# Two store and load cuts in a dilated 3x3 convolution: the first pair's stores regrouped, the eighth pair's load halved

## The chip, the cores and the metric

The kernel runs on one core of a Trainium2 chip. The metric is the device time of one execution in microseconds (us); several executions are made in rounds, the kernel before and the other kernel on the same chip. Two kernels count as the same when they are within 2%. All ratios below are ratios of means: the mean time of one kernel's fast runs over the mean of the other's fast runs of the same rounds, so a ratio is not quite the ratio of the medians quoted beside it. Runs over 1.5% above the fastest of the same kernel are left out of the ratios. They are not left out of the medians: where a median contains one, it is a little high.

## The reference, cut to what matters

```python
batch, c_in, h, w, c_out, k, dilation = 16, 64, 64, 64, 128, 3, 2      # float32
x_pad = np.pad(x, ((0, 0), (0, 0), (2, 2), (2, 2)))
# for all b, co, ci, kh, kw:
output[b, co] += weight[co, ci, kh, kw] * x_pad[b, ci, kh*2:kh*2+h, kw*2:kw*2+w]
```

The input is 16.8 MB, the output 33.6 MB. Nearly all of both has to cross between HBM and the on-chip memory once.

## The kernel before

Two images make a pair, because 2 x 64 input channels fill the 128 partitions. There are 8 pairs. One load brings a pair (128 partitions x 64 rows x 64 columns, 2 MB). Each pair is computed in four groups `g` of 16 rows; `G` counts all 32 groups. ACT casts the input to fp16, DVE forms row sums, PE does the products (with sums shared between rows), DVE adds them into the output tile `osb`. An output tile holds both images of a pair: 128 output channels x 2 images x 4096 values, 4 MB. There are three input buffers and three output buffers. All loads and stores are issued by SP, in program order, so they form one queue.

```python
    def load(pb, cuts=(0, H)):
        x32_tiles[pb] = fpool.tile([P, HW], f32, tag="x32", name="x32")
        for lo, hi in zip(cuts[:-1], cuts[1:]):
            nc.sync.dma_start(
                out=x32_tiles[pb][:, lo * W : hi * W], in_=x_pair[pb, :, lo * W : hi * W]
            )
    # ... cut: casts, row sums, weights; ahead of the loop load(0), load(1), load(2)

    def store(pb, m, r0=0, r1=H, rows=((0, P),)):
        for lo, hi in rows:
            nc.sync.dma_start(
                out=out_img[2 * pb + m, lo:hi, r0 * W : r1 * W],
                in_=o_tiles[pb][lo:hi, m * HW + r0 * W : m * HW + r1 * W],
            )

    FOUR = ((0, P - 4), (P - 4, P))
    ROWS4 = 8

    for G in range(ngroups):
        # ... cut: the products and the sums of group g of pair pb
        if G == 0:
            load(XF)                                   # XF = 3
        if g == NG - 1 and 0 < pb < npairs - XF - 1:
            load(pb + XF + 1)
        if pb in (0, npairs - 1):
            if g % 2 == 1:
                store(pb, 0, (g - 1) * GR, (g + 1) * GR)
                if pb and g == 1:
                    store(pb, 1, 0, 2 * GR - ROWS4)
                    store(pb, 1, 2 * GR - ROWS4, 2 * GR, FOUR)
                else:
                    store(pb, 1, (g - 1) * GR, (g + 1) * GR)
            if G == NG - 1:
                load(XF + 1)
        elif g == NG - 1:
            store(pb, 0)
            store(pb, 1)
```

So the first pair is stored in four transfers of 1 MB (rows 0 to 31 of each image after the second group, rows 32 to 63 after the fourth), and every later pair but the last in two transfers of 2 MB.

## Time and profile before

| | before |
|---|---|
| time | 126.86 us (126.79 to 127.05, 3 runs) |
| span of the profiled run | 125.0 us |
| PE's last matmul ends | 107.8 us |
| DVE's last addition ends | 109.1 us |
| moved by DMA | 50.8 MB, 406 GB/s over the span |

The page of the profile, kernel before. In the second block each character or number is one of 40 slices of 3.1 us: the mean busy share of the 16 DMA engines in tenths, and what they moved in GB/s.

```profile
span 125.0 us, 2339 instructions
...
DMA  4999999899999999999999999999999999999991
GB/s 145 373 427 456 435 420 399 299 425 422 446 438 430 425 420 440 422 430 420 435 425 433 430 430 430 420 425 425 446 430 425 430 420 425 425 433 411 424 387 76
DMA packets 4466, 50.78 MB, mean 406 GB/s; under 512 B 488, under 2 KB 488, under 8 KB 1000
...
PE 76%; DMA 6%; ACT 2%; DVE 1%; DVEq 1%; SPq 1%; issue 0%
```

The two readings seem to disagree. The chain of waits follows the work back from the last instruction, and gives PE 76%. But nothing computes after 109.1 us, and the span ends at 125.0. In those 16 us the DMA engines write out what was queued, at about the rate that they have had since the third slice. The chain follows releases between instructions; a queue that always has a backlog does not appear in it as a wait. The DMA row is the one to read here: apart from the first and the last slice it is at nine tenths throughout, with one weak slice, the eighth (299 GB/s).

The DMA issues of SP around the places that the change touches, kernel before (timeline of SP; a row can merge several issues, and its duration then runs to the end of the last of them):

```profile
16.62 7.04 SPq L185 DMA_DIRECT2D out_dram<-osb  x4
23.76 0.61 SPq L64 DMA_DIRECT2D x<-in_x_dram  x1
...
54.70 0.34 SPq L64 DMA_DIRECT2D x<-in_x_dram  x1
```

Two of the four stores are issued at 16.6 us and two at 22.6. The fifth load follows at 23.8.

### The profile page before, as it was taken

To read this page: it belongs to the slowest core of one execution; us is meant where nothing else is said; L and a number is where in the kernel's file an instruction comes from. 1 tells how busy PE (TensorE), PEld (TensorE's weight loads), DVE (VectorE), ACT (ScalarE), POOL (GpSimd) and SP (SyncE) were. 2 spreads that over 40 slices of the span, in tenths; PEclk is the share of its full clock that TensorE was granted. 3 is DMA by queue.
4 is the path that set the end of the run, shared out by engine and by line. 5 is a ranking of instruction groups with operands and counts; after the bars stand their busy time and mean duration, and the time that the engine had idled before them with its cause. 6 is when DMAs were issued, how large, how long until landed. Compare 5 with 4: busy or idle time off the path is not lost.

```text
span 125.0 us, 2339 instructions
## 1 busy us (share of the span) xinstructions
PE 105.1 (84%) x1000; PEld 56.0 (45%) x1000; DVE 90.8 (73%) x103; ACT 64.9 (52%) x68; POOL 2.2 (2%) x8
## 2 busy tenths in 40 slices
PE   6996999999999999999999999999999999400000
PEld 2252555555555555555555555555555555200000
DVE  0562998988898888988988898888988987700000
ACT  4287996665666566656665666566653333000000
POOL 2400000000000000000000000000000000000000
PEclk9999999999999999999999999999999999985555
DMA  4999999899999999999999999999999999999991
GB/s 145 373 427 456 435 420 399 299 425 422 446 438 430 425 420 440 422 430 420 435 425 433 430 430 430 420 425 425 446 430 425 430 420 425 425 433 411 424 387 76
DMA packets 4466, 50.78 MB, mean 406 GB/s; under 512 B 488, under 2 KB 488, under 8 KB 1000
## 3 DMA queue, kind: packets, MB, share of 16 engines
q1 hardware_dynamic: 4456, 50.63, 96.6%
q8 instruction: 8, 0.13, 0.4%
q14 instruction: 2, 0.02, 0.0%
HBM read 17.07 MB, written 33.55 MB: 405 GB/s over the span
## 4 chain that ended last, share of the span: by engine, by line
PE 76%; DMA 6%; ACT 2%; DVE 1%; DVEq 1%; SPq 1%; issue 0%
PE psA L171 31%; PE psB L171 30%; PE psP L171 16%; DMA x<-in_x_dram 6%; ACT x L73 2%; DVE osb L234 1%; DVEq L290 1%; ACT p_sb L227 1%; SPq L64 0%; SPq L88 0%; DVEq L234 0%
## 5 line engine op out<-in xcount | busy, mean ns | idle before, releaser
L171 PEld LDWEIGHTS <-w_sb 64*128 64x128 f16 x960 | 53.9, 94 | 46.6 <-issue 1.5
L227 ACT COPY p_sb<-psP 128x1024 f32<-128x1024 f32 x32 | 32.4, 1012 | 36.8 <-issue 21.6
L234 DVE TENSOR_TENSOR osb<-psA,p_sb 128x1024 f32<-128x1024 f32 x32 | 39.2, 1224 | 13.6 <-PE psA L171 9.0
L171 PE MATMUL psA<-x,w_sb 64*128 64x496 f16 (+3 forms) x384 | 45.0, 365 | 0.0
L171 PE MATMUL psB<-x,w_sb 64*128 64x496 f16 (+3 forms) x384 | 45.0, 365 | 0.0
L234 DVE TENSOR_TENSOR osb<-psB,p_sb 128x1024 f32<-128x1024 f32 x32 | 39.0, 1220 | 0.0
L73 ACT CAST x<-x 128x1024 f16<-128x1024 f32 (+2 forms) x31 | 32.1, 1044 | 0.6 <-DMA x<-in_x_dram 0.5
L171 PE MATMUL psP<-xs,w_sb 64*128 64x496 f16 (+1 forms) x192 | 26.0, 371 | 1.2 <-ACT p_sb L227 1.2
L85 DVE TENSOR_TENSOR xs<-x 128x512 f16<-128x512 f16 x32 | 13.3, 415 | 0.6 <-ACT x L73 0.6
L101 PE MATMUL dm<-zero 128*128 128x512 f16 x10 | 4.6, 580 | 1.2 <-DVE zero L93 1.2
L111 DVE CAST wd<-w 128x192 f16<-128x192 f32 x1 | 0.5, 502 | 2.4 <-DMA w<-in_weight_dram 2.4
L101 PEld LDWEIGHTS <-zero 128*128 128x128 f16 x10 | 1.1, 124 | 2.6 <-issue 1.3
L124 PEld LDWEIGHTS <-wd 128*64 128x64 f16 x30 | 1.0, 118 | 2.2 <-DVE wd L111 1.1
L124 PE MATMUL wt<-ident,wd 128*64 128x128 f16 x30 | 1.6, 241 | 0.2 <-DVE wd L111 0.2
L113 ACT ACT_TABLE_LOAD x1 | 1.3, 1283 | 0.7 <-PEq L276 0.7
L136 ACT CAST w_sb<-wt 128x384 f16<-128x384 f32 x1 | 0.5, 479 | 1.9 <-PE wt L124 1.9
L113 ACT CAST wd<-w 128x192 f16<-128x192 f32 x1 | 0.5, 537 | 1.6 <-DMA w<-in_weight_dram 1.6
L138 DVE CAST w_sb<-wt 128x384 f16<-128x384 f32 x1 | 0.6, 557 | 0.9 <-PE wt L124 0.9
L93 DVE MEMSET zero<- 128x256 uint32 x1 | 0.3, 272 | 0.9 <-PEq L276 0.9
L112 POOL TENSOR_TENSOR wd<-w 128x192 f16<-128x192 f32 x1 | 0.8, 792 | 2.3 <-DMA w<-in_weight_dram 2.3
L115 POOL CAST wd<-w 128x192 f16<-128x192 f32 x1 | 0.8, 803 | 0.0
L114 DVE TENSOR_TENSOR wd<-w 128x192 f16<-128x192 f32 x1 | 0.8, 780 | 0.0
(11 smaller groups left out, 3.6 us busy)
## 6 DMA issues: line engine op xcount, KB each, us to landing
out_dram<-osb SPq DMA_DIRECT2D x12, 2048.0 KB, 19.3
x<-in_x_dram SPq DMA_DIRECT2D x7, 2048.0 KB, 17.6
out_dram<-osb SPq DMA_DIRECT2D x7, 1024.0 KB, 13.5
x<-in_x_dram SPq DMA_DIRECT2D x1, 1088.0 KB, 5.3
x<-in_x_dram SPq DMA_DIRECT2D x1, 960.0 KB, 7.1
out_dram<-osb SPq DMA_DIRECT2D x1, 768.0 KB, 15.9
w<-in_weight_dram SPq DMA_DIRECT2D x1, 288.0 KB, 2.8
out_dram<-osb SPq DMA_DIRECT2D x1, 248.0 KB
```

Source lines behind the costliest of these rows:

```text
L73: nc.scalar.copy(out=x16_tiles[pb][:, lo * W : hi * W], in_=x32_tiles[pb][:, lo * W : hi * W])
L85: nc.vector.tensor_tensor(out=s, in0=v[:, :, 0], in1=v[:, :, 1], op=add)
L101: nc.tensor.matmul(out=dm[:, 0:512], lhsT=zero[:, 0:P], rhs=zero)
L112: nc.gpsimd.tensor_tensor(out=wdv[:, 3], in0=wv[:, 0], in1=wv[:, 1], op=sub)
L113: nc.scalar.copy(out=wdv[:, 2], in_=wv[:, 0])
L114: nc.vector.tensor_tensor(out=wdv[:, 1], in0=wv[:, 2], in1=wv[:, 1], op=sub)
L115: nc.gpsimd.tensor_copy(out=wdv[:, 4], in_=wv[:, 2])
L124: nc.tensor.matmul(out=wts[k % 3][r * CI : (r + 1) * CI, c0 + j * CO : c0 + (j + 1) * CO], lhsT=wd[:, t * CI : (t + 1) * CI], rhs=ident,)
L171: nc.tensor.matmul(out=po, lhsT=w_sb[pp, t * CO : (t + 1) * CO], rhs=rhs, start=first and j == 1, stop=last and j == 2,)
L227: nc.scalar.copy(out=p_sb, in_=psP)
L234: nc.vector.tensor_tensor(out=o[:, :, b0 : b0 + NBLK, e], in0=ps.rearrange("p (m b q) -> p m b q", m=2, q=2 * W), in1=pv, op=add,)
L290: with _tile.TileContext(nc) as tc:
```

## The change

The intent, as it can be read from the source: store the first pair in fewer and mostly larger transfers (1.5 MB for rows 0 to 47 of each image, then 1 MB for rows 48 to 63 of both images together), and cut the eighth pair's load in two, so that its first half can be issued, and land, before the second.

```diff
+    def store_both(pb, r0, r1):
+        nc.sync.dma_start(
+            out=out_img[2 * pb : 2 * pb + 2, :, r0 * W : r1 * W].rearrange("m o q -> o m q"),
+            in_=o_tiles[pb].rearrange("p (m q) -> p m q", m=2)[:, :, r0 * W : r1 * W],
+        )
# ... cut
         if g == NG - 1 and 0 < pb < npairs - XF - 1:
-            load(pb + XF + 1)
-        if pb in (0, npairs - 1):
+            load(pb + XF + 1, (0, H) if pb < 3 else (0, H // 2, H))
+        if G == NG - 2:
+            store(0, 0, 0, (NG - 1) * GR)
+            store(0, 1, 0, (NG - 1) * GR)
+        if G == NG - 1:
+            store_both(0, (NG - 1) * GR, H)
+            load(XF + 1)
+        elif pb == npairs - 1:
             if g % 2 == 1:
                 store(pb, 0, (g - 1) * GR, (g + 1) * GR)
-                if pb and g == 1:
+                if g == 1:
# ... cut: the last pair's stores are unchanged
-            if G == NG - 1:
-                load(XF + 1)
```

## The prediction

> **What bounds the kernel now.** The chain of waits puts 76% of the span on PE, but PE's work ends near 106.7 us and DVE's at 108.0; the span is 125.0. The last 17 us are the DMA queue emptying. The 40 slices show the DMA engines nine tenths busy from the third on, mostly at 420 to 446 GB/s, 50.8 MB in all. The Trainium skill ("DMA: Bandwidth & Descriptors", "Where 436 GB/s comes from") gives a ceiling of 435 GB/s; the stretches 30 to 60 us show 428 to 433, so it agrees. The packets' time is 121.4 us per engine, and the first byte moves at 2.3 us. So the kernel is one saturated queue: its bytes plus three losses: the start, a dip (slice 8, 299 GB/s: about 21.3 to 23.9 us, when the last packets of the fourth load take up to 1.2 us instead of 0.61; 0.96 us of excess per engine), and a tail in which the engines end unevenly, the last some 4 us after the first.
>
> **What the change does, costed by the packet records.** A packet of 8 KB takes 309 ns, one of 16 KB 611: about 7 ns plus 37.75 ns per KB. My estimates from these are 158 ns for 4 KB and 460 for 12 KB.
> - First pair's stores: 512 packets of 8 KB (512 x 309 / 16 = 9.89 us of 16 engines) become 256 of 12 KB and 256 of 4 KB (256 x 618 / 16 = 9.89 us). No difference. Four issues become three, on a sequencer that is idle there.
> - The combined store has 128 partitions as its slowest dimension; the skill (same page, "How many engines (k)") says that such a transfer uses 16 engines. I expect the full rate.
> - Eighth load: 128 packets of 16 KB (4.89 us) become 256 of 8 KB (4.94 us): +0.06 us. One issue more. Its first half waits for only half of the casts that free the buffer, so it can be issued some 6 us before 54.7.
> - Moved: the first stores are issued at about 19.5 us instead of 16.6. By then the queue still holds the fourth load, which lands at about 24 us, so it does not run dry; the second store still comes at 22.6, before the fifth load at 23.8: the queue's order is unchanged. The eighth load took 20.6 us from issue to landing, behind a long backlog; issuing half of it earlier changes no order either.
>
> **On the critical path** (the queue): +0.06 us, and whatever happens to the dip and to the unevenness at the end, each of which could move by half a microsecond. If the dip came from the early stores waiting behind the load it would shrink; I think it more likely stays.
>
> **Prediction.** 126.7 us, 125.9 to 127.4 eight times in ten. Faster by over 2%: 0.02; within 2%: 0.96; slower: 0.02.
>
> **What would show it.** Right: DMA busy nine tenths through 18 to 30 us with no hole, the combined store landing about as late as its predecessors did (near 34 us), PE's end unmoved near 106.7, slice 8 still low. Wrong: a hole in the DMA row before the first stores, the combined store slow or on few engines, DVE waiting longer for out_dram<-osb (0.5 us now), or slice 8 at 420 GB/s (then about 1 us faster).
>
> **What would make it wrong.** The halves or the later stores shifting the engines against each other, so that the tail gets longer or shorter; or 4 KB packets being slower than estimated.

## More of the kernel before

The timeline of the end, kernel before (start, duration, engine, line, operation):

```profile
106.49 1.29 PE L171 MATMUL psB<-x,w_sb 64*128 64x512 f16 x12
...
107.91 1.21 DVE L234 TENSOR_TENSOR osb<-psB,p_sb 128x1024 f32<-128x1024 f32 x1
109.16 0.93 SPq L185 DMA_DIRECT2D out_dram<-osb  x2
```

## The result, and the profile after

| | before | after |
|---|---|---|
| time | 126.87 us (126.79 to 127.05, 4 runs) | 126.68 us (126.53 to 126.85, 4 runs) |
| ratio of the fast runs | 1 | 0.9984, 95% interval 0.9965 to 1.0002 |
| span of the profiled run | 125.0 us | 125.1 us |
| DVE's last addition ends | 109.1 us | 109.3 us |

The kernel takes the same time. The page of the kernel after:

```profile
span 125.1 us, 2339 instructions
...
DMA  4999999999999999999999999999999999999981
GB/s 123 389 457 430 435 430 419 377 430 397 438 434 430 367 424 424 432 445 419 435 419 404 417 445 435 430 430 435 424 424 424 430 424 440 430 409 411 428 379 66
DMA packets 4594, 50.78 MB, mean 406 GB/s; under 512 B 488, under 2 KB 488, under 8 KB 1256
...
PE 76%; DMA 6%; ACT 2%; DVE 1%; DVEq 1%; SPq 1%; issue 0%
```

The DMA row has no hole, the bytes and the mean rate are the same, and there are 128 packets more. The eighth slice rose from 299 to 377 GB/s, and the fourteenth fell from 425 to 367. The issues of SP, kernel after:

```profile
19.63 0.83 SPq L185 DMA_DIRECT2D out_dram<-osb  x2
22.73 0.38 SPq L191 DMA_DIRECT2D out_dram<-osb  x1
23.22 1.17 SPq L64 DMA_DIRECT2D x<-in_x_dram  x1
...
54.87 1.36 SPq L64 DMA_DIRECT2D x<-in_x_dram  x2
```

The first stores are issued 3 us later than before, the last of the first pair at the same time (22.7 us). The first half of the eighth load is issued at 54.87 us, not earlier than the whole load was (54.70): both halves wait for the release of the whole buffer. In the trace SP's wait ends with ACT's last cast of the fifth pair (53.91 to 54.85 us), whose buffer this is; the second cast, which finishes the first half, had ended at 48.77.

### A ledger of the queue

The trace records each DMA packet with its start, its duration and its size. From these records I worked out, for each kernel's profiled run, the terms of the queue's length, in us per DMA engine (sums over all packets divided by 16). "Nominal" takes each packet of data (and of the few instruction fetches) at the median duration of its size in that run. "Excess" is what these packets took above that (differences of 9 ns and more). "Length" runs from the start of the first data packet to the end of the last. "Idle" is the length less the recorded time of all packets. It is a net figure: the records overlap a little, so from 48 to 100 us, where the queue has no hole, they add up to 1.007 of the engines' time in the kernel before and to 1.022 in small_packets. The small rest up to "length" is semaphore writes. The first data packet starts 1.74 to 1.76 us into the span in every run. "Excess 19 to 47" is the part of the excess in that stretch.

| kernel | nominal | excess | idle | length | excess 19 to 47 |
|---|---|---|---|---|---|
| before | 118.76 | 2.21 | 0.82 | 122.07 | 1.09 |
| before_again | 118.76 | 1.99 | 0.84 | 121.87 | 0.68 |
| halves_only | 118.82 | 2.08 | 0.65 | 121.83 | 0.96 |
| after | 118.83 | 2.12 | 0.92 | 122.16 | 0.96 |
| after_again | 118.83 | 2.08 | 0.77 | 121.97 | 0.82 |
| stores_only | 118.78 | 2.32 | 0.89 | 122.26 | 1.07 |
| small_packets | 121.23 | 2.02 | -0.36 | 123.33 | 0.86 |
| whole_at_4th | 118.70 | 3.25 | 1.57 | 123.81 | 1.87 |
| late_hole | 118.70 | 3.18 | 2.01 | 124.16 | 1.82 |
| load4_late_before | 118.76 | 3.14 | 0.63 | 122.81 | 1.71 |
| load4_late_after | 118.91 | 3.26 | 5.16 | 127.59 | 1.94 |
| slower_pe | 118.76 | 3.27 | 2.57 | 124.89 | 1.08 |
| slower_pe_half | 118.76 | 3.09 | 1.66 | 123.80 | 1.04 |
| rows12 | 118.82 | 2.73 | 2.01 | 123.85 | 1.36 |

Of the 125 us, 118.8 are packets at their ordinary pace. The change adds 0.07 to that and leaves the other terms within their scatter.

### The profile page after: what moved, and what is told of

It reads as the page before. It is cut to its first block, busy times and chain, and to the rows that moved or that the text cites. A ratio compares the mean times of both kernels' runs of the same rounds, so it can differ in the third digit from the quotient of the medians.

```text
span 125.1 us, 2339 instructions
## 1 busy us (share of the span) xinstructions
PE 104.6 (84%) x1000; PEld 56.7 (45%) x1000; DVE 91.0 (73%) x103; ACT 65.0 (52%) x68; POOL 2.2 (2%) x8
## 4 chain that ended last, share of the span: by engine, by line
PE 76%; DMA 6%; ACT 2%; DVE 1%; DVEq 1%; SPq 1%; issue 0%
PE psA L171 31%; PE psB L171 30%; PE psP L171 16%; DMA x<-in_x_dram 6%; ACT x L73 2%; DVE osb L240 1%; DVEq L300 1%; ACT p_sb L233 1%; SPq L64 0%; SPq L88 0%; DVEq L240 0%
## 5 line engine op out<-in xcount | busy, mean ns | idle before, releaser
L171 PEld LDWEIGHTS <-w_sb 64*128 64x128 f16 x960 | 54.6, 94 | 46.3 <-issue 1.6
L240 DVE TENSOR_TENSOR osb<-psA,p_sb 128x1024 f32<-128x1024 f32 x32 | 39.2, 1225 | 13.5 <-PE psA L171 9.4
L101 PE MATMUL dm<-zero 128*128 128x512 f16 x10 | 4.1, 533 | 1.2 <-DVE zero L93 1.2
L146 ACT CAST x<-x 128x512 f16<-128x512 f32 x1 | 0.6, 618 | 0.5 <-DMA x<-in_x_dram 0.5
```

The costliest lines, as they stand in the source:

```text
L101: nc.tensor.matmul(out=dm[:, 0:512], lhsT=zero[:, 0:P], rhs=zero)
L171: nc.tensor.matmul(out=po, lhsT=w_sb[pp, t * CO : (t + 1) * CO], rhs=rhs, start=first and j == 1, stop=last and j == 2,)
L240: nc.vector.tensor_tensor(out=o[:, :, b0 : b0 + NBLK, e], in0=ps.rearrange("p (m b q) -> p m b q", m=2, q=2 * W), in1=pv, op=add,)
```

## The experiments

The theory: the time is the length of one saturated queue; the change keeps the bytes, the packets' time and the absence of holes, so it is worth nothing. The rivals: the change's two parts have effects that cancel; the first -0.2 us is a real gain; or PE bounds the kernel and the queue does not.

### The kernel before against itself

No edit.

> The kernel before, unchanged, run as its own rival: the noise of the comparison. Every theory expects a ratio of 1.000 within 0.2%. The dip: if it belongs to the first load with stores behind it, this trace has it again near 21 to 23 us with about 0.9 us of excess packet time per engine; if it falls anywhere by chance, it is elsewhere, smaller or missing.

Measured: 126.77 us against 126.93, ratio 0.9984 (0.9960 to 1.0009). A kernel compared with itself thus gives the same 0.9984 as the change did. The first -0.2 us is not more than the noise. The dip is there again at the same place, with about half the size (0.49 us of excess from 19 to 26 us against 0.96 in the first profile): it belongs to the place, but its size varies from run to run.

### The changed kernel again

No edit.

> The changed kernel again, with more rounds. Theory (one saturated queue, same packet time): 0.997 to 1.001 of before. Rival (the -0.2 us seen at first is a real gain): 0.998 or less with an interval clear of 1. Rival (two effects cancel): also about 0.998 here, but the two halves of the change apart from it differ from 1 in opposite directions by over 0.3%.

Measured: 126.79 us against 126.93, ratio 0.9997 (0.9960 to 1.0033). The theory holds; no gain is resolved.

### The stores alone, and the halves alone

```diff
# stores_only: the changed kernel with
-            load(pb + XF + 1, (0, H) if pb < 3 else (0, H // 2, H))
+            load(pb + XF + 1)
# halves_only: the kernel before with
-            load(pb + XF + 1)
+            load(pb + XF + 1, (0, H) if pb < 3 else (0, H // 2, H))
```

> Only the first pair's stores as in the change; the eighth load whole. Theory: 9.89 us of packet time per engine as before, no hole in the DMA row, ratio 0.997 to 1.001. Rival (cancelling effects): clearly faster, under 0.997, with the halves costing it back.

> Only the eighth load in halves; the first pair stored as before. Theory: +0.06 us of packet time per engine, ratio 0.999 to 1.002. Rival (cancelling effects): slower by over 0.3%.

Measured: stores_only 126.70 us, ratio 0.9966 (0.9935 to 0.9998); halves_only 127.00 us, ratio 1.0001 (0.9976 to 1.0027). The ratio of stores_only is 0.0004 below the theory's range, and its interval lies just below 1, which by the letter is the rival's side. But the queue of its profiled run is not shorter (122.26 us), the halves do not cost it back, and the whole change, run beside it, is at 0.9997. Both intervals overlap that of the kernel against itself, so no effect of either part is shown, and no pair of large cancelling effects; a gain of the stores of some tenths of a percent is not excluded. The ledger gives the two parts' cost in packet time: +0.02 and +0.06 us.

There is, however, a cancellation inside the stores. The six profiles make two families. The busy times of two stretches (columns: the stretch and its length, busy time of PE, PEld, DVE, ACT and POOL with their instructions, granted clock, DMA share, GB/s). First the three kernels that store the first pair as before; this is the kernel before:

```profile
20.00:24.00 4.00, 4.00 (x44) 2.26 (x41) 3.65 (x4) 3.05 (x3) 0.00 (x0) 1.00 0.95 305
39.00:44.00 5.00, 5.00 (x50) 2.63 (x48) 4.58 (x5) 2.46 (x4) 0.00 (x0) 1.00 1.01 429
```

The same of before_again:

```profile
20.00:24.00 4.00, 4.00 (x44) 2.36 (x42) 3.41 (x5) 3.05 (x4) 0.00 (x0) 1.00 0.97 360
39.00:44.00 5.00, 5.00 (x51) 2.73 (x48) 4.58 (x5) 2.47 (x4) 0.00 (x0) 1.00 1.01 423
```

The same of halves_only:

```profile
20.00:24.00 4.00, 4.00 (x45) 2.30 (x42) 3.50 (x4) 3.05 (x4) 0.00 (x0) 1.00 0.96 324
39.00:44.00 5.00, 5.00 (x52) 2.66 (x48) 4.58 (x5) 2.46 (x4) 0.00 (x0) 1.00 1.03 436
```

Then the three with the change's stores; this is the kernel after:

```profile
20.00:24.00 4.00, 4.00 (x45) 2.30 (x41) 3.48 (x4) 3.15 (x4) 0.00 (x0) 1.00 0.99 386
39.00:44.00 5.00, 5.00 (x52) 2.66 (x49) 4.58 (x5) 2.46 (x4) 0.00 (x0) 1.00 0.98 374
```

The same of after_again:

```profile
20.00:24.00 4.00, 4.00 (x45) 2.30 (x42) 3.41 (x5) 3.05 (x4) 0.00 (x0) 1.00 0.96 382
39.00:44.00 5.00, 5.00 (x52) 2.66 (x48) 4.58 (x5) 2.47 (x4) 0.00 (x0) 1.00 1.02 406
```

The same of stores_only:

```profile
20.00:24.00 4.00, 4.00 (x44) 2.36 (x42) 3.41 (x6) 3.05 (x4) 0.00 (x0) 1.00 1.01 393
39.00:44.00 5.00, 5.00 (x50) 2.73 (x48) 4.26 (x5) 2.83 (x4) 0.00 (x0) 1.00 0.99 374
```

In the first stretch the fourth load ends and the first stores begin; in the second, the sixth load ends and the second pair's stores begin. With the old stores the last packets of the fourth load are slow and those of the sixth are not (305 to 360 GB/s, then 423 to 436). With the new stores the fourth load is less slow and the sixth is slow too (382 to 393, then 374 to 406). From the profiles of before and after: 4 us x (386 - 305) GB/s = 0.32 MB more moved in the first stretch, 5 us x (429 - 374) = 0.28 MB less in the second. At 425 GB/s that is 0.76 us gained and 0.65 us given back. DMA shares near 1 show that the engines were not idle in either stretch; the packets themselves were slower (a 16 KB packet takes 611 ns at the median, and up to 2 us there).

The place of the dip goes with the time at which the first stores are issued. At 16.6 to 16.9 us (before, before_again, halves_only, and slower_pe below) 0.5 to 1.0 us of excess lies between 20 and 24 us and at most 0.11 between 39 and 44. At 19.6 to 20.2 us (after, after_again, stores_only) it is 0.3 to 0.4 and 0.4 to 0.6. In the profiled run of rows12 (below), which is the changed kernel up to 100 us but came late by chance, they are issued at 21.05 us, and it is 0.04 and 0.87. Two runs below do not fall in line: slower_pe_half (18.7 us) is still at 0.89 and 0.05, and small_packets (19.5 us), whose second pair is stored in other packets, at 0.63 and 0.11. No experiment varied this time alone, and why the packets are slow, none settles.

### Is PE the bound?

```diff
# slower_pe: the kernel before with
-        for j in (1, 0, 2):
+        for n, j in enumerate((1, 1, 0, 2) if kind == 0 else (1, 0, 2)):
# ... cut
-                    stop=last and j == 2,
+                    stop=last and j == 2 or kind == 0 and n == 0,
# slower_pe_half: the same, in the odd groups G alone
```

> The kernel before, but two matmuls of each of the 32 summed products are done twice (the first result is overwritten, the output stays right). It adds about 0.2 us of PE to each group, 6 to 7 us in all, so PE ends near 113 instead of 106.7 us. Theory (the DMA queue is the bound, PE has room): 126.5 to 127.3 us. Rival (PE bounds, as 76% of the chain of waits would say): about 133 us.

Measured: 129.44 us, ratio 1.0199 (1.0179 to 1.0219): +2.6 us. Neither number came. The stores of the seventh pair in the timeline of SP, kernel before:

```profile
96.78 0.90 SPq L185 DMA_DIRECT2D out_dram<-osb  x2
```

The busy times just after, kernel before:

```profile
100.00:105.00 5.00, 5.00 (x50) 2.63 (x48) 4.17 (x6) 1.16 (x2) 0.00 (x0) 1.00 0.99 423
```

The same stores in slower_pe:

```profile
102.94 0.81 SPq L185 DMA_DIRECT2D out_dram<-osb  x2
```

The same stretch of busy times in slower_pe:

```profile
100.00:105.00 5.00, 5.00 (x54) 2.85 (x50) 4.07 (x5) 1.29 (x2) 0.00 (x0) 1.00 0.74 315
```

The stores came 6.2 us later, and the queue ran dry for about 1.1 us per engine between 100 and 105 us (worked out from the packet records). So the slack of the computation there is about 5 us, an estimate from these two numbers (6.2 - 1.1). It is not the 16 us by which the computation ends ahead of the queue. The ledger has the rest: 1.06 us more excess, 0.7 of it from 116 us on, where the kernel before has none, and a more uneven end. The queue is the bound, but PE is not far behind it.

> As slower_pe, but only every other group does the two extra matmuls: about 3.4 us more PE in all instead of 6.8. slower_pe took 2.6 us more, with the queue dry for 1.1 us per engine near 103 us, because the seventh pair's stores came at 102.9 instead of 96.8. Theory (PE has a slack of about 5 us at that point, and below it costs nothing): 126.5 to 127.3 us and no hole. Rival (PE's time counts in part everywhere, 2.6 of 6.8): about 128.1 us.

Measured: 127.50 us, ratio 1.0044 (0.9998 to 1.0090): the same by the 2% rule, but it does not decide between theory and rival. Two of the four runs came at 126.84 and 127.04 us, as the theory says, and two at 127.96 and 128.51, nearer to the rival. The profile is of the 128.51 run, and in it PE began slowly. The first products in the timeline, kernel before:

```profile
7.24 1.29 PE L171 MATMUL psA<-x,w_sb 64*128 64x512 f16 x12
```

The same in slower_pe_half:

```profile
8.63 2.13 PE L172 MATMUL psA<-x,w_sb 64*128 64x512 f16 x12
```

In that run the first stores were issued at 18.7 us instead of 16.6, so a delay of 2 us from the start came on top of the added 3.4. The seventh pair's stores came at 101.92 us, 5.1 later than before, and the queue was dry there for 0.35 us per engine. That puts the slack at 4.8 us, close to the 5 of slower_pe. (The rest of that run's loss is again slow packets from 115 us on, 0.6 us, and a more uneven end.) The Trainium skill ("TensorE: Matmul & The Clock Gate", "What's actually happening") says that the warm-up of PE's clock varies from run to run, since the window that watches its activity runs freely. This trace agrees that it varies: its first record of PE's clock, at full rate, stands at 10.38 us, against 5.57 in the kernel before, and 12 matmuls ahead of it took 2.13 us instead of 1.29. (The column of granted clock reads 1.00 there only because it counts time without a record as full.) Two traces thus support a slack of about 5 us; that a delay below it costs nothing, the four runs do not prove.

### When do later stores cost something?

```diff
# whole_at_4th: the changed kernel with
-        if G == NG - 2:
-            store(0, 0, 0, (NG - 1) * GR)
-            store(0, 1, 0, (NG - 1) * GR)
         if G == NG - 1:
-            store_both(0, (NG - 1) * GR, H)
+            store(0, 0)
+            store(0, 1)
             load(XF + 1)
# late_hole: the same three lines under "if G == NG + 1:"
```

> The changed kernel, but the first pair is stored whole, 2 MB an image, after its fourth group (issue near 22.6 us instead of 19.6). Theory (the queue has the fourth load until 22.9 to 23.4 us, and a transfer starts about 1 us after its issue): no hole or one of at most 0.7 us, 126.4 to 127.5 us. Rival (storing the first pair early is worth something in itself): about 3 us more, the delay of the stores.

Measured: 128.62 us, ratio 1.0131 (1.0101 to 1.0160), over the theory's range by 1.1 us. One stretch of its busy times:

```profile
22.00:24.00 2.00, 2.00 (x23) 1.14 (x20) 1.83 (x3) 1.90 (x2) 0.00 (x0) 1.00 0.65 279
```

There is a hole: share 0.65, and 0.7 us per engine without a packet in the records, the upper end of what was expected. The ledger names what was not expected: the excess rose by 1.04 us against before. From 19 to 26 us, where the fourth load ends, it all but vanished (0.05 us instead of 0.96), but from 26 to 47 us it rose from 0.13 to 1.82, at the turns from the first pair's stores to the fifth load and from the sixth load to the next stores. So 3 us later than the change puts them, the stores cost 1.8 us against the kernel before: the hole, and more slow packets.

> The changed kernel, but the first pair is stored whole only after the sixth group (about 28.7 us), and the fifth load is issued behind it. Now the queue must run dry from about 23 us to 29.5. Theory: the time grows by the hole, 5.5 to 6.8 us, to 132 to 133.7 us, though PE and DVE end where they did. Rival (the backlog of some 15 us at the end absorbs a hole, or PE bounds): about 127 us.

Measured: 128.66 us, ratio 1.0137 (1.0105 to 1.0169). The experiment was built wrong. SP waits only for the data that a store reads, and the first pair's data are ready after the fourth group wherever the store stands in the program; nothing earlier in SP's queue held it back. The trace shows the stores issued at 23.27 us and not at 28.7. SP's program is that of whole_at_4th, and so is the time. The run counts as a repeat of it, and the long hole went untested here.

> The kernel before, but the fourth load is issued behind the first two stores (about 17.5 us) instead of at 10.7. The three loads ahead of it keep the queue busy until about 18 us, so it does not run dry. Theory (only a hole in the queue costs time, not the moment of the stores as such): 126.4 to 127.5 us. Rival (the order of loads and stores matters by itself): over 128 us.

> The changed kernel with the same edit: the fourth load behind its first two stores, so both are issued from 19.6 us on. The three loads end near 18 us and a transfer starts about 1 us after its issue: a hole of about 2.6 us. Theory: 129.0 to 130.4 us, and the trace shows the hole. Rival (a hole early in the run is absorbed, since the queue has a backlog later): as the kernel before with that edit, within 0.5 us.

```diff
-        if G == 0:
-            load(XF)
# load4_late_before: in the kernel before, behind the stores of G == 1
+            if G == 1:
+                load(XF)
# load4_late_after: in the changed kernel, behind the stores of G == NG - 2
+            load(XF)
```

Measured: load4_late_before 128.43 us (a median with one slow run in it), ratio 1.0141 (1.0085 to 1.0197), its fast runs 127.50, 127.70 and 129.16; load4_late_after 130.71 us, ratio 1.0317 (1.0269 to 1.0366). The busy times of load4_late_after:

```profile
18.00:20.00 2.00, 2.00 (x22) 1.12 (x20) 1.91 (x3) 2.00 (x3) 0.00 (x0) 1.00 0.04 8
20.00:22.00 2.00, 2.00 (x22) 1.03 (x19) 1.67 (x3) 1.58 (x3) 0.00 (x0) 1.00 0.00 0
```

Here is a real hole, and it is not absorbed: 4.1 us per engine in the profiled run. That was the run of 132.28 us, in which PE also began slowly and the stores were issued at 21.4 us; the other three took 130.54 to 130.84. In the ledger the queue is 5.5 us longer than before: 4.3 of idle and 1.05 of excess. The span of the same run is 5.5 us longer too (130.5 against 125.0). A hole early in the run is paid in full, as the theory says, but the kernel's time (130.71 us, and 130.54 at the least) lies above its range; the slow packets were not in the sum.

load4_late_before misses the theory's range; of its fast runs only that of 127.50 us, the profiled one, is on its edge. Its idle time is not larger than before (0.63 against 0.82), but its excess is 0.93 larger. The busy times of one stretch, kernel before:

```profile
22.00:30.00 8.00, 8.00 (x82) 4.32 (x78) 7.00 (x9) 5.67 (x6) 0.00 (x0) 1.00 0.92 371
```

The same stretch of load4_late_before:

```profile
22.00:30.00 8.00, 8.00 (x82) 4.37 (x78) 7.00 (x9) 5.63 (x6) 0.00 (x0) 1.00 1.01 346
```

The order of loads and stores thus matters by itself, without a hole, by 0.7 us of queue length in this fastest run (122.81 against 122.07): the engines are busy (1.01) but slow. In this kernel a load stands between the first pair's stores, so the queue turns between loads and stores twice more. The theory in its first form ("only a hole costs time") falls; the queue's length also depends on how many packets are slow.

### Does the packets' size count?

```diff
# small_packets: the changed kernel, pairs two to seven
-            store(pb, 0)
-            store(pb, 1)
+            for k in range(NG):
+                store_both(pb, k * GR, (k + 1) * GR)
```

> The changed kernel, but pairs two to seven are stored in four combined transfers each of 16 rows of both images, at the same moment as before: 4 KB packets for 16 KB ones. From the measured packets: 6144 x 159 / 16 = 61.1 us of engine time instead of 1536 x 611 / 16 = 58.7. Theory (the time is the sum of the packets' time): +2.4 us, with the extra issues up to +2.9: 128.9 to 129.8 us. Rival (packet size does not matter from 4 KB up, bytes alone count): 126.5 to 127.1 us.

Measured: 129.14 us, ratio 1.0179 (1.0140 to 1.0219), in the theory's range: the size of the packets counts, and the rival falls. The sum behind the range was not right, though. Nominal time did rise by 2.40 us against the changed kernel (121.23 - 118.83), since a 4 KB packet is recorded at 159 ns and a 16 KB packet at 611. But the queue of the profiled run is only 1.2 us longer (123.33 against 122.16). The busy times of a stretch in which only stores move, kernel after:

```profile
80.00:95.00 15.00, 15.00 (x148) 8.29 (x146) 13.10 (x16) 8.84 (x9) 0.00 (x0) 1.00 1.01 429
```

The same stretch of small_packets:

```profile
80.00:95.00 15.00, 15.00 (x150) 8.20 (x146) 12.94 (x16) 8.84 (x9) 0.00 (x0) 1.00 1.03 419
```

The records of the small packets overlap more (1.03 against 1.01), so their durations overstate their cost; 25.2 MB at 419 instead of 429 GB/s is 1.4 us, an estimate from these two rates. A further 0.7 us of the span lies behind the last data packet (1.84 us instead of 1.16): there SP, whose closing waits begin with the store that lands last, still works through five of them, in the kernel after through one. That the time met the range is thus partly luck, and the profiled run (128.70 us) was the fastest of the four. In the change itself 4 KB packets are paired with 12 KB packets (460 ns), which is why they cost nothing there: 159 + 460 = 619 ns of recorded time, against 2 x 309 = 618 for two of 8 KB.

### A try at the end of the queue

```diff
# rows12: the changed kernel with
-    ROWS4 = 8
+    ROWS4 = 12
```

> The changed kernel, with 12 rows instead of 8 of the last pair's second image sent through the two transfers of 124 and 4 partitions. A try at the uneven end of the engines. If the few engines that these transfers use end early, as the source seems to assume, up to 0.3 us less: 126.3 to 126.6 us; if they are already level, up to 1.2 us more. No theory of the change depends on it.

Measured: 128.55 us, ratio 1.0137 (1.0104 to 1.0170): +1.6 us. The Trainium skill ("DMA: Bandwidth & Descriptors", "Why a DMA increments its semaphore by 16 and not by 1", under "How many engines (k)") states that a transfer uses the largest number of engines up to 16 that divides its slowest dimension; for 124 and for 4 partitions that is 4. Those four engines then get 32 packets of 121 ns instead of 84, an estimate of 32 x 37 = 1.2 us more, from the packet records; the transfer ahead of them shrinks by 8 packets of 38 ns, 0.3 us, on every engine. The trace agrees: from 123.5 to 124.6 us just four packets are under way at a time. Twelve engines that wait 1.2 us are 0.9 us of idle time per engine, and it rose by 1.1 (2.01 - 0.92). The excess of that run was 0.6 us higher as well, 0.4 of it before 47 us, ahead of anything that the edit changes: the first record of PE's clock is late (9.38 us) and the first stores came at 21.05 us. With 8 rows the end is better balanced than with 12; this leads to no faster kernel, and no other experiment does.

## Why the prediction was right

- **126.7 us, same.** It held: 126.68 at first, 126.79 again. The reason given held too: bytes, packet time and holes are unchanged. That the number was met to 0.1 us is luck, since runs of one kernel lie 0.3 us and more apart.
- **The queue is the bound.** It held. 4.3 us more of idle time, nearly all one hole of 4.1, and slow packets of 1.05 us made the span 5.5 us longer (load4_late_after), and a queue longer by 1.2 us, with a slower end of the program, made the span of small_packets 1.8 us longer than the changed kernel's. With PE's end 7.0 us later (114.8 instead of 107.8 us) the kernel took only 2.6 us more (slower_pe). What I read as PE's distance was too generous: the computation is about 5 us ahead at the seventh pair, not 16.
- **The packets.** 158 and 460 ns were estimated for 4 and 12 KB; the trace has 159 and 460. The ledger gives +0.02 us for the stores and +0.06 for the halves; predicted were 0 and +0.06. As small_packets shows, such sums of durations are good for the direction and not for the last tenth.
- **The combined store on 16 engines, at full rate.** It fits. The table of slices shows no weak slice while it runs (397, 438 and 434 GB/s from 28 to 37.5 us; its packets lie between 30.0 and 35.9), and one engine alone moves 16 KB in 611 ns, which is 27 GB/s. It landed 13.5 us after its issue, at 36.24 us. Its two predecessors, issued at 22.6 and 22.9 us, landed at 34.15 and 36.48, so it was about as late as the second of them; the 34 of the prediction is the first alone.
- **No hole through 18 to 30 us.** It held; the moved stores had room. DVE's wait for out_dram<-osb went from 0.5 to 0.7 us, little beside its slack of about 5. whole_at_4th shows that 3 us more would have used it up.
- **The half load issued 6 us earlier: wrong.** Both halves came at 54.87 us. The buffer is released as a whole. Nothing followed from it, since a long backlog stood ahead of the load.
- **The dip stays: half wrong.** I gave the eighth slice as "still low", and 420 GB/s there as worth 1 us. It went from 299 to 377, which would have been most of that gain; it was given back at the sixth load (slice 14, 425 to 367). The step that failed is the treatment of the dip as one event that stays or goes. It is a slowness that the order of the transfers can move, and its sum over 19 to 47 us is alike in the two families (0.68 to 1.09 us before and in halves_only, 0.82 to 1.07 in the three with the new stores, 1.36 in rows12 whose stores came later still).
- **Times misread.** The packet times that the prediction quotes (first byte, dip, end of the engines) are about 0.55 us too late, since I took the wrong origin for the records: the first data packet starts at 1.74 us and the dip is at about 20.8 to 23.4. The ends given for PE and DVE are about 1 us too early; they are where the chain of waits leaves them, not their last instructions. Neither changed the argument.

## What to carry to other kernels

When the DMA row is full from beginning to end, the time is bytes over rate plus holes plus slow packets, whatever the chain of waits says. Regrouping transfers is then worth what it changes in those three terms, and the first two can be estimated from the packets before the change is built: the holes from the times of issue, the packets' time only roughly (2.4 us by recorded durations were 1.2 to 1.4 in the queue here). The slow packets could not be foreseen here. Before expecting anything from moving a transfer, ask whether the queue would have been empty without it, and look further down the queue for the place where a local gain is given back.

## What the Trainium skill lacked or had wrong

- "DMA: Bandwidth & Descriptors" has nothing on slow packets near the turn from loads to stores: 16 KB packets of 611 ns took up to 2.3 us there, 0.7 to 1.4 us per engine between 19 and 47 us in the usual runs and 1.7 to 1.9 with another order of transfers or with later stores. The cause is open.
- The same page ("Specifications") gives 512 B as the smallest transfer for line rate. Here, above it, the size of a packet still counts: stores in 4 KB packets moved at 419 GB/s, in 16 KB packets at 429 (80 to 95 us of small_packets and after). The recorded durations, 84 ns for 2 KB, 159 for 4 KB and 611 for 16 KB, fit about 7 ns plus 37.75 ns per KB, but they overlap and overstate the difference.
- The same page ("Latency and other measured facts") gives about 0.6 us to the first byte and does not say from when. Here the first data packet started 1.0 us after the start of the first issue, that of the weights (0.74 to 1.74 us), and 0.62 us after its end; for a store on an empty queue it was 0.85 and 0.50 us (load4_late_after, issue at 21.37, first packet at 22.22 us). The figure fits if it is counted from the end of the issue.
- "TensorE: Matmul & The Clock Gate" ("What's actually happening") puts the ramp's penalty under 1% of a typical kernel's span. In three of the fourteen profiled runs here the first clock record came at 9.4 to 10.4 us instead of 3.9 to 6.4, and the first stores 1.4 to 1.8 us later than in a like kernel, over 1% of some 126 us (slower_pe_half, 18.73 us against 16.94 in slower_pe; load4_late_after, 21.37, and rows12, 21.05, against 19.63 in after). What this cost in time was not measured apart; the load4_late_after run in question took 132.28 us, the other three 130.54 to 130.84.
